# A ConvFFN trunk in float32: scaled activations from pair 6 on, and 22 pairs with seven products in place of 17

## The chip, the cores and the metric

The kernel runs on one core of a Trainium2 chip. The metric is the device time in microseconds of one execution; it is 1045.43 us before the change, the median of three runs (1045.23 to 1045.83). All data are float32, and every large matrix product is computed to nearly float32 accuracy.

## The reference

The model is an encoder trunk of two layers on 512 positions and 1024 channels. Only the second half of a layer, the ConvFFN, is touched by the change.

```python
for l in range(DEPTH):            # 2
    h = rmsnorm(x, norm1[l])
    ...
    x = x + mix @ w_o[l]

    h = rmsnorm(x, norm2[l])
    up = dwconv_centred(h @ w_up[l], conv_w[l], conv_b[l])   # 1024 -> 2 * 2816, width 3 over positions
    gate, val = up[..., :D_FF], up[..., D_FF:]
    x = x + (jax.nn.silu(gate) * val) @ w_down[l]            # 2816 -> 1024
```

The norm is x times g times a factor per position, 1 / sqrt(mean(x^2) + eps). The factor depends on the position alone, so it may be applied before the product with w_up or after it.

## The kernel before

**Layout.** Activations stand transposed: channels on the 128 partitions, the 512 positions along the free dimension. x is eight tiles x0 to x7 of 128x512. The normed input of the FFN is `h2`, eight tiles with the tag act, which hold x times norm2 without the factor of the position. The factor is a row `rb2` (tag rb), the same on all partitions; it is made last, after x is complete, from a sum of squares: `col_rstd`, then `row_rstd`, whose transposes on PE are line 242 of the profile.

**Three products for one.** Each operand is split into a high half of reduced precision and a low rest (`split`; for weights `wsplit`, tiles whi and wlo, five buffers each). The high half is a copy on ScalarE (ACT, line 94), the rest a subtraction on VectorE (DVE, line 97). `mm3` issues high x high, low x high and high x low (lines 124, 125, 126) on TensorE (PE). So each weight block costs ACT and DVE one instruction each before PE can go on. Raw weights come in loads of 512 KB into wraw, three buffers, issued by SP.

**The FFN.** The 5632 columns of w_up make 44 tiles of 128, taken as 22 pairs: gate tile fi and value tile fi + 22. The pairs stand in six groups (`GROUPS`); the down projection of a group (`rows`, eight pieces, each one output tile of x: one split of weights, 3 x 4 matmuls of 512 columns, or 3 x 3 in a group of three, and an addition to x) is interleaved with the pairs of the next group. A pair is computed in one of two ways.

- `up_eight`: two halves, gate and value, each with two splits of weights and 24 matmuls of 512 columns into one PSUM bank, then one multiplication by rb2 out of PSUM into a tile tF.
- `up_seven`: gate and value tile together as a 2 x 2 block product with seven products in place of eight, in the manner of Strassen and Winograd. It has seven splits of weights, four sums of weights (s1 to s4, into `sums` and back into wraw), 84 matmuls of 256 columns, and sums of partial results out of PSUM. On the other side it needs sums of the blocks of h, T1 to T4, which `seven_h` builds once a layer for each of four pairs of h2 tiles: two additions of halves, four sums of 256 columns, two splits into spare tiles (`h_rooms`, which hands out tiles that earlier stages of the layer have done with). At the end it multiplies by rb2: one instruction of 512 columns, two of 256.

`conv` applies the convolution over positions to the result: one ACT instruction for the centre tap and the bias, and two scalar-tensor-tensor instructions on DVE for the outer taps (line 100). SiLU runs on ACT, gate times value on DVE, and the result is split into high and low for the down projection (tiles slab and pT).

`SEVEN` lists the pairs of each layer that use `up_seven`: 7 in layer 0, 10 in layer 1. In layer 0 the same loop also prepares weights of layer 1 (`presplit`, tiles tA and m4, stored to DRAM as `kept`); `PIECES` says how many pieces each pair does.

**Order.** The program is written in this order, and a scheduler of the framework then decides each engine's instruction order from its own estimate of times, within the dependences. Each engine works through its own list in order, so an instruction that waits holds up those behind it.

## Time and profile before

| | |
|---|---|
| median of three timed runs | 1045.43 us |
| profiled execution, whole | 1045.6 us |
| its span on the core | 1043.8 us |
| PE busy | 1025.7 us, 98% |
| DVE busy | 857.2 us, 82% |
| ACT busy | 546.9 us, 52% |
| granted TensorE clock | 1.0 |

A row of the timeline reads: start in the span, duration, engine, line, operation, output<-inputs (the program's names without their numbers), shape, and in brackets how long the engine stood idle just before it and what ended that. A row of the groups reads: line, engine, operation, names, shapes and count, then busy time and mean ns of one, then the idle time just before them and what ended it. Durations of PE and DVE rows overlap the next row, so the distance from start to start is what an instruction costs its engine.

In the profiled execution rb2 is ready at about 201 us in layer 0 and 716 us in layer 1; the FFN's pairs follow.

### The profile page before, as it was taken

How to read it: one execution, taken by the hardware profiler on the slowest of the kernel's cores; microseconds unless marked ns; L12 is line 12 of the kernel's file. 1: busy time of each engine (PE TensorE's matmuls, PEld its weight loads, DVE VectorE, ACT ScalarE, POOL GpSimd, SP SyncE). 2: the span in 40 equal slices, each digit the busy share in tenths (PEclk: the TensorE clock that was granted, in tenths of full speed). 3: DMA queues.
4: the chain of work that ended last, by engine and by line, in shares of the span. 5: the costliest groups of instructions: out<-in, count | busy, mean ns of one | idle time of the engine just before them, and what ended most of it. 6: DMA issues, size and time to landing. Idle time of an engine off the chain costs nothing.

```text
span 1043.8 us, 16032 instructions
## 1 busy us (share of the span) xinstructions
PE 1025.7 (98%) x5696; PEld 888.4 (85%) x5696; DVE 857.2 (82%) x1721; ACT 546.9 (52%) x1057; POOL 61.1 (6%) x142
## 2 busy tenths in 40 slices
...
GB/s 270 89 109 68 41 93 82 116 171 189 162 199 139 196 202 207 188 200 243 226 206 219 111 62 91 132 85 98 81 101 101 115 69 134 63 127 57 111 137 81
DMA packets 64325, 140.15 MB, mean 134 GB/s; under 512 B 6386, under 2 KB 22002, under 8 KB 64244
## 3 DMA queue, kind: packets, MB, share of 16 engines
...
q14 instruction: 36, 0.29, 0.1%
...
## 4 chain that ended last, share of the span: by engine, by line
PE 90%; DVE 6%; ACT 2%; issue 1%; DMA 0%; POOL 0%; ACTq 0%; DVEq 0%; POOLq 0%
PE ps L124 27%; PE ps L126 27%; PE ps L125 27%; PE ps L122 3%; PE ps L667 2%; PE ps L660 2%; PE ps L648 1%; DVE tF L100 1%; DVE wlo L97 1%; ACT tA L94 1%; PE ps L242 1%; DVE tF L97 1%; PE ps L235 1%; DVE tA L652 1%; DVE x L97 0%
## 5 line engine op out<-in xcount | busy, mean ns | idle before, releaser
L94 ACT ACTIVATE whi<-wraw 128x512 fp32r<-128x512 f32 (+1 forms) x313 | 187.9, 614 | 230.9 <-PE ps L126 139.9
L125 PE MATMUL ps<-act,wlo 128*128 128x512 f32 (+1 forms) x700 | 250.1, 359 | 0.4 <-DVE wlo L97 0.4
L124 PE MATMUL ps<-act,whi 128*128 128x512 f32 (+1 forms) x700 | 250.5, 359 | 0.0
L126 PE MATMUL ps<-act,whi 128*128 128x512 f32 (+1 forms) x700 | 249.8, 359 | 0.0
L97 DVE TENSOR_TENSOR wlo<-wraw,whi 128x512 fp32r<-128x512 f32 (+1 forms) x321 | 210.0, 668 | 41.7 <-ACT whi L94 41.0
L125 PEld LDWEIGHTS ps<-act,wlo 128*128 128x128 f32 x700 | 132.0, 189 | 21.1 <-DVE wlo L97 1.1
L124 PEld LDWEIGHTS ps<-act,whi 128*128 128x128 f32 x700 | 132.0, 189 | 19.8
L126 PEld LDWEIGHTS ps<-act,whi 128*128 128x128 f32 x700 | 132.0, 189 | 19.2
L100 DVE SCALAR_TENSOR_TENSOR tF<-tF,pb,tF 128x511 f32<-128x511 f32 x176 | 130.2, 746 | 3.9 <-ACT tF L94 3.7
L124 PE MATMUL ps<-slab,whi 128*128 128x512 f32 (+2 forms) x274 | 105.8, 389 | 1.2 <-ACT whi L94 1.2
L125 PE MATMUL ps<-slab,wlo 128*128 128x512 f32 (+2 forms) x274 | 104.6, 382 | 0.0
L97 DVE TENSOR_TENSOR x<-x,ps 128x512 f32<-128x512 f32 (+1 forms) x113 | 75.2, 677 | 34.3 <-PE ps L126 34.0
L126 PE MATMUL ps<-slab,whi 128*128 128x512 f32 (+2 forms) x274 | 102.2, 383 | 0.3 <-DVE slab L97 0.3
L94 ACT ACTIVATE tF<-tF,pb 128x512 f32<-128x512 f32 x88 | 71.1, 811 | 29.7 <-DVE tF L97 28.0
L97 DVE TENSOR_TENSOR tF<-ps,rb 128x512 f32<-128x512 f32 (+1 forms) x87 | 54.4, 634 | 23.5 <-PE ps L126 12.2
L124 PE MATMUL ps<-room,whi 128*128 128x256 f32 x238 | 67.5, 283 | 1.1 <-ACT tF L94 1.0
L125 PE MATMUL ps<-room,wlo 128*128 128x256 f32 x238 | 67.2, 282 | 0.3 <-DVE wlo L97 0.3
L126 PE MATMUL ps<-room,whi 128*128 128x256 f32 x238 | 67.0, 282 | 0.0
L124 PE MATMUL ps<-pT,whi 128*128 128x512 f32 (+1 forms) x162 | 62.6, 388 | 0.0
L125 PE MATMUL ps<-pT,wlo 128*128 128x512 f32 (+1 forms) x162 | 62.6, 388 | 0.0
L126 PE MATMUL ps<-pT,whi 128*128 128x512 f32 (+1 forms) x162 | 61.7, 387 | 0.0
L124 PEld LDWEIGHTS ps<-slab,whi 128*128 128x128 f32 x274 | 51.5, 188 | 11.4 <-ACT whi L94 1.6
...
## 6 DMA issues: line engine op xcount, KB each, us to landing
...
```

The lines of the kernel that those rows point to most:

```text
L94: return nc.scalar.activation(out, in_, func, **kw)
L97: return (eng or nc.vector).tensor_tensor(out, a, b, op=op)
L100: return nc.vector.scalar_tensor_tensor(out=out, in0=a, scalar=s, in1=b, op0=op0, op1=op1)
L122: nc.tensor.matmul(out, a[0], b[0], start=start, stop=stop, **kw)
L124: nc.tensor.matmul(out, a[0], b[0], start=start, stop=False, **kw)
L125: nc.tensor.matmul(out, a[1], b[0], start=False, stop=False, **kw)
L126: nc.tensor.matmul(out, a[0], b[1], start=False, stop=stop, **kw)
L235: nc.tensor.matmul(pt[:, 2 * b:2 * b + 2], acc[:, b * P:(b + 1) * P], ones2, start=True, stop=True)
L242: nc.tensor.matmul(pt[:, b * P:(b + 1) * P], r[:, b:b + 1].to_broadcast([P, P]), ident, start=True, stop=True)
L648: nc.tensor.matmul(sc[:, :n], qT[p][:, e, i * P:(i + 1) * P], kT[g][:, s, j0 * P:(j1 + 1) * P], start=s == 0, stop=s == 1)
L660: tr = nc.tensor.transpose(pp[:, j * P:(j + 1) * P], pr[:, j * P:(j + 1) * P], ident)
L667: pv = nc.tensor.matmul(py[64 * e:64 * e + 64, i0 * P:(i1 + 1) * P], vp[:, j, 64 * g:64 * g + 64], pT[:, half, e, b0:b0 + 2 * (i1 - i0) + ...
```

## The change

The norm's factor goes into h itself from pair 6 on. At the start of the FFN eight new tiles `hx` take the sum of each h2 tile's halves; the code multiplies them by rb2 after pairs 2 and 3; after pair 5 the h2 tiles are split anew from hx. From pair 6 (`SCALED`) `up_eight` hands out its PSUM tile as it is, and `conv` reads PSUM three times; `up_seven` leaves out its three multiplications by rb2 and copies one block of 256 columns out of PSUM on ACT. `seven_h` takes its blocks from hx, without the two additions, and is called twice after pair 4 and twice after pair 6 (before: twice at the start, and after pairs 3 and 4). The lists of pairs with seven products grow from 7 to 10 in layer 0 and from 10 to 12 in layer 1, and the pieces of presplit are spread otherwise. At the value half of pair 5 two pieces of the down projection are taken.

```diff
--- before.py
+++ after.py
@@ -35,8 +35,10 @@
 
 GROUPS = [(0, 4), (4, 4), (8, 4), (12, 3), (15, 3), (18, 4)]
 
-PIECES = [1, 1, 2, 1, 2, 2, 2] + [1, 3] * 7 + [3]
-SEVEN = ((7, 9, 11, 13, 15, 17, 19), (6, 8, 9, 11, 12, 14, 15, 17, 18, 20))
+SCALED = 6
+
+PIECES = [1, 1, 1, 1, 1, 1, 2, 3, 1, 2, 3, 2, 1, 3, 2, 2, 3, 2, 2, 3, 2, 2]
+SEVEN = ((8, 9, 11, 12, 14, 15, 17, 18, 20, 21), (8, 9, 10, 12, 13, 14, 15, 17, 18, 19, 20, 21))
 
 
 def encoder_kernel(tc, t):
@@ -402,24 +404,26 @@
         for key, cols in zip(keys, (LO, HI)):
             g[key] = [z[:, cols] for z in two]
 
+    HX = ("th0", "th1", "tl0", "tl1", "wt0", "wt1", "v", "accA")
+
     def h_rooms():
 
-        for tag in ("th0", "th1", "tl0", "tl1", "wt0", "wt1", "v", "accA", "accF", "acc", "room"):
+        for tag in ("accF", "room"):
             yield cp.tile([P, 512], F32R, tag=tag, name=nm("room"), bufs=1)
+        for _ in range(2):
+            yield tp.tile([P, 516], F32R, tag="tail", name=nm("room"), bufs=2)[:, :512]
+        yield cp.tile([P, 512], F32R, tag="acc", name=nm("room"), bufs=1)
         yield cp.tile([P, 512], F32R, tag="rb", name=nm("room"), bufs=2)
         for _ in range(2):
-            yield tp.tile([P, 516], F32R, tag="tail", name=nm("room"), bufs=2)[:, :512]
-        for _ in range(2):
             yield temp(512, "sq", F32R)
-
-    def seven_h(k, h2, room):
-
-        b = [temp(512, "tF") for _ in range(2)]
-        for i in range(2):
-            tt(b[i], f(h2[k + 4 * i][:, 0, :]), f(h2[k + 4 * i][:, 1, :]), ALU.add)
+        for k in (0, 4, 1, 5, 2, 6, 3, 7):
+            yield cp.tile([P, 512], F32R, tag=HX[k], name=nm("room"), bufs=1)
+
+    def seven_h(k, h2, hx, room):
+
         g = dict(B11=[z[:, LO] for z in halves(h2[k])], B21=[z[:, LO] for z in halves(h2[k + 4])],
                  B22=[z[:, HI] for z in halves(h2[k + 4])])
-        t13, t24 = sums_of_b(*b)
+        t13, t24 = sums_of_b(hx[k], hx[k + 4])
         parts(g, t13, ("T1", "T3"), room)
         parts(g, t24, ("T2", "T4"), room)
         return g
@@ -432,9 +436,11 @@
             for k in range(KT):
                 mm3(o, [q[:, (k % 4) * P:(k % 4 + 1) * P] for q in w[k // 4]], [h2[k][:, s, :] for s in range(2)],
                     k == 0, k == KT - 1)
-            u = temp(512, "tF")
-            tt(u, o, rb2, ALU.mult)
-            yield u
+            if fi < SCALED:
+                u = temp(512, "tF")
+                tt(u, o, rb2, ALU.mult)
+                o = u
+            yield o
 
     def up_seven(l, fi, h2, ts, rb2):
         a, b = [wload(t["w_up"][l, fi + z * FT], 1024) for z in range(2)]
@@ -465,11 +471,9 @@
         product(X, wsplit(s3), "T3")
         tt(ub[:, HI], ub[:, HI], X, ALU.add)
         tt(ua[:, HI], ua[:, HI], Y, ALU.add)
-        tt(ua, ua, rb2, ALU.mult)
         yield ua
         product(X, wsplit(a22), "T4")
-        tt(ub[:, LO], X, rb2[:, LO], ALU.mult)
-        tt(ub[:, HI], ub[:, HI], rb2[:, HI], ALU.mult)
+        act(ub[:, LO], X)
         yield ub
 
     def conv(l, m, u):
@@ -829,7 +833,10 @@
 
         ahead = presplit(l + 1) if l < L - 1 else iter(lambda: 0, 1)
         room = h_rooms()
-        ts = [seven_h(k, h2, room) for k in range(2)]
+        hx = [cp.tile([P, 512], F32, tag=z, name=nm("hx"), bufs=1) for z in HX]
+        for k in range(KT):
+            tt(hx[k], f(h2[k][:, 0, :]), f(h2[k][:, 1, :]), ALU.add)
+        ts = []
         nxt = []
 
         def rows(f0, nf, gu):
@@ -865,12 +872,18 @@
                 ys_ = []
                 for z, u in enumerate((up_seven if fi in SEVEN[l] else up_eight)(l, fi, h2, ts, rb2)):
                     ys_.append(conv(l, fi + z * FT, u))
-                    for _ in range(-(-todo // halves_left)):
+                    for _ in range(2 if z and fi == SCALED - 1 else -(-todo // halves_left)):
                         next(down, None)
                         todo -= 1
                     halves_left -= 1
-                if fi in (3, 4):
-                    ts.append(seven_h(len(ts), h2, room))
+
+                for k in range(4 * fi - 8, 4 * fi - 4) if fi in (2, 3) else ():
+                    tt(hx[k], hx[k], rb2, ALU.mult)
+                if fi == SCALED - 1:
+                    for k in range(KT):
+                        split(h2[k][:, 0, :], h2[k][:, 1, :], hx[k])
+                for _ in range(2 if fi in (4, SCALED) else 0):
+                    ts.append(seven_h(len(ts), h2, hx, room))
                 for _ in range(PIECES[fi]):
                     next(ahead)
                 act(ys_[0], ys_[0], AF.Silu)
```

The scheduler moves instructions as well. Lines of the changed program are two higher in the helpers (99 for 97, 102 for 100, 126 to 128 for 124 to 126), numbers behind names count tiles and belong to one program alone. Three places follow.

**Behind rb2 in layer 0, on DVE.** Before, the first product of rb2 (rb_418) with a PSUM tile, and what came with it:

```order
L97 TENSOR_TENSOR wlo_515_2270<-wraw_513_2267,whi_514_2269 128x512
L97 TENSOR_TENSOR tF_441_1964<-ps_440_1939,rb_418_1891 128x512
L97 TENSOR_TENSOR tF_449_2005<-ps_448_1980,rb_418_1891 128x512
L97 TENSOR_TENSOR wlo_517_2274<-wraw_513_2267,whi_516_2273 128x512
L97 TENSOR_TENSOR tF_463_2059<-ps_462_2034,rb_418_1891 128x512
L100 SCALAR_TENSOR_TENSOR tF_442_1966<-tF_441_1964,pb_96,tF_442_1966 128x511
```

After it the convolution of the first pair began. In the changed program the first such product (tF_433<-ps_432) is followed by seven multiplications of hx tiles, and then by these rows:

```order
L99 TENSOR_TENSOR hx_425_1899<-hx_425_1899,rb_418_1891 128x512
L99 TENSOR_TENSOR wlo_504_2248<-wraw_500_2241,whi_503_2247 128x512
L99 TENSOR_TENSOR hx_426_1900<-hx_426_1900,rb_418_1891 128x512
L99 TENSOR_TENSOR tF_441_1985<-ps_440_1960,rb_418_1891 128x512
L102 SCALAR_TENSOR_TENSOR tF_434_1946<-tF_433_1944,pb_96,tF_434_1946 128x511
L99 TENSOR_TENSOR wlo_516_2304<-wraw_514_2301,whi_515_2303 128x512
L99 TENSOR_TENSOR wlo_518_2308<-wraw_514_2301,whi_517_2307 128x512
```

All eight multiplications of hx by rb2 now stand between the first PSUM tile's and the second's, with one split of weights among them.

**Pair 5 to pair 6 in layer 0, on DVE.** Before, in the order of the program, the additions of the previous group's down pieces to x, a sum for T parts, and the low halves of the weights of a down piece (wlo_596) and of the next pair (wlo_609, wlo_611, wlo_617):

```order
L97 TENSOR_TENSOR x1_75<-x1_75,ps_556_2445 128x512
L97 TENSOR_TENSOR x2_76<-x2_76,ps_586_2547 128x512
L97 TENSOR_TENSOR tF_559_2463<-tF_558_2460,tF_557_2459 128x256
L97 TENSOR_TENSOR wlo_596_2603<-wraw_583_2541,whi_595_2602 128x512
L97 TENSOR_TENSOR wlo_609_2645<-wraw_607_2642,whi_608_2644 128x512
L97 TENSOR_TENSOR wlo_611_2649<-wraw_607_2642,whi_610_2648 128x512
L97 TENSOR_TENSOR wlo_617_2686<-wraw_615_2683,whi_616_2685 128x512
```

The changed program has the same down piece as wlo_579 and the next pair as wlo_588 and wlo_590. The low halves of the eight h2 tiles, split anew, stand in the 24 rows ahead of them, the last two here:

```order
L99 TENSOR_TENSOR act_408_1849<-hx_425_1899,act_408_1849 128x512
L99 TENSOR_TENSOR x1_75<-x1_75,ps_536_2407 128x512
L99 TENSOR_TENSOR x2_76<-x2_76,ps_565_2509 128x512
L99 TENSOR_TENSOR act_412_1871<-hx_426_1900,act_412_1871 128x512
L99 TENSOR_TENSOR wlo_579_2585<-wraw_577_2582,whi_578_2584 128x512
L99 TENSOR_TENSOR wlo_588_2635<-wraw_586_2632,whi_587_2634 128x512
```

So all eight low halves are written ahead of the down piece's weights.

On PE the down piece (ps_597) and the first product of pair 6 (ps_612, which reads the h2 tile act_370) stood thus before:

```order
L124 MATMUL ps_597_2606<-slab_456_2021,whi_595_2602 128x512
L124 MATMUL ps_612_2652<-act_370_1689,whi_608_2644 128x512
L124 MATMUL ps_618_2689<-slab_456_2021,whi_616_2685 128x512
L125 MATMUL ps_597_2606<-slab_456_2021,wlo_596_2603 128x512
L126 MATMUL ps_597_2606<-slab_456_2021,whi_595_2602 128x512
```

and the changed program has, with ps_580 for the down piece and ps_591 for pair 6:

```order
L126 MATMUL ps_580_2588<-slab_448_2001,whi_578_2584 128x512
L126 MATMUL ps_591_2642<-act_370_1689,whi_587_2634 128x512
L126 MATMUL ps_595_2675<-slab_448_2001,whi_593_2671 128x512
L127 MATMUL ps_580_2588<-slab_448_2001,wlo_579_2585 128x512
L128 MATMUL ps_580_2588<-slab_448_2001,whi_578_2584 128x512
```

PE's order is the same here. Between rb2's transposes and the first use of the down piece's low half PE has 209 matmuls of 512 columns in the changed program's layer 0 and 201 in its layer 1.

**A seven pair late in layer 1, on DVE.** Before, the end of pair 17 (tF_2164 is its gate tile, tF_2165 its value tile) with multiplications by rb2 (rb_1680), and splits and sums of weights of pair 18:

```order
L97 TENSOR_TENSOR tF_2165_10103<-tF_2165_10103,ps_2161_10099 128x256
L100 SCALAR_TENSOR_TENSOR tF_2179_10212<-tF_2164_10102,pb_96,tF_2179_10212 128x511
L97 TENSOR_TENSOR wlo_2202_10305<-wraw_2192_10277,whi_2201_10304 128x512
L97 TENSOR_TENSOR x7_81<-x7_81,ps_2189_10259 128x512
L97 TENSOR_TENSOR tF_2165_10103<-tF_2165_10103,rb_1680_7567 128x256
L97 TENSOR_TENSOR wlo_2204_10322<-wraw_2191_10275,whi_2203_10321 128x512
L97 TENSOR_TENSOR wlo_2206_10340<-sums_2200_10301,whi_2205_10339 128x512
L97 TENSOR_TENSOR tF_2165_10103<-ps_2161_10099,rb_1680_7567 128x256
L97 TENSOR_TENSOR wraw_2191_10275<-wraw_2191_10275,sums_2200_10301 128x512
L100 SCALAR_TENSOR_TENSOR tF_2186_10251<-tF_2165_10103,pb_96,tF_2186_10251 128x511
```

The changed program at the same place (tF_2169 is the value tile of pair 17, tF_2200 the gate tile of pair 18):

```order
L99 TENSOR_TENSOR tF_2169_10260<-tF_2169_10260,ps_2165_10256 128x256
L99 TENSOR_TENSOR x7_81<-x7_81,ps_2193_10414 128x512
L99 TENSOR_TENSOR wlo_2206_10460<-wraw_2196_10432,whi_2205_10459 128x512
L99 TENSOR_TENSOR wlo_2208_10477<-wraw_2195_10430,whi_2207_10476 128x512
L99 TENSOR_TENSOR wlo_2210_10495<-sums_2204_10456,whi_2209_10494 128x512
L99 TENSOR_TENSOR wraw_2195_10430<-wraw_2195_10430,sums_2204_10456 128x512
L102 SCALAR_TENSOR_TENSOR tF_2190_10406<-tF_2169_10260,pb_96,tF_2190_10406 128x511
L99 TENSOR_TENSOR tF_2200_10437<-tF_2200_10437,ps_2199_10436 128x256
L99 TENSOR_TENSOR wlo_2212_10513<-wraw_2195_10430,whi_2211_10512 128x512
```

The rows with rb are gone; the first tap (tF and pb) has only the sum out of PSUM ahead of it.

In the whole program 128x512 matmuls go from 2732 to 2492 and 128x256 matmuls from 1708 to 2128. On DVE the additions for hx, the multiplications of hx by rb2 and the low halves of the new split are 16 each over both layers; 16 additions of seven_h, 30 multiplications of a whole PSUM tile by rb2, and all 17 + 17 + 17 of the seven pairs go; each of the five more seven pairs has four sums and three splits of weights more, and the taps that read PSUM are 40. On ACT the copies of 256 columns out of PSUM go from 51 to 88, and the splits of weights by 15 more.

## The prediction

> **What bounds the kernel now.** I read the page's first part, its chain of work that ended last, then the windows, then the timeline of PE and of DVE, and last the groups of instructions by form.
>
> ```profile
> span 1043.8 us, 16032 instructions
> PE 1025.7 (98%) x5696; PEld 888.4 (85%) x5696; DVE 857.2 (82%) x1721; ACT 546.9 (52%) x1057; POOL 61.1 (6%) x142
> PE 90%; DVE 6%; ACT 2%; issue 1%; DMA 0%; POOL 0%; ACTq 0%; DVEq 0%; POOLq 0%
> ```
>
> PE carries 90% of the chain that ends last, DVE 6%. The change lies in the FFN alone, so the FFN's own windows count, one over most of layer 0's and one late in layer 1's (columns: stretch, its length, busy PE, PEld, DVE, ACT, POOL, granted clock, DMA share, GB/s; the third row counts only instructions that touch the tA tiles, which presplit uses):
>
> ```profile
> 202.00:470.00 268.00, 267.14 (x1444) 231.92 (x1443) 249.79 (x447) 147.57 (x259) 0.00 (x0) 1.00 0.56 184
> 850.00:875.00 25.00, 25.00 (x161) 22.77 (x160) 21.43 (x38) 13.13 (x23) 0.00 (x0) 1.00 0.41 126
> 202.00:470.00 268.00, 0.00 (x0) 0.00 (x0) 30.81 (x71) 19.54 (x35) 0.00 (x0) 1.00 0.56 184
> ```
>
> PE is full in both at a granted clock of 1.00; DVE is close behind at 249.79/268 = 93% in layer 0, where presplit takes 30.81/22 pairs, at least 1.3 us a pair, and at 86% late in layer 1. So two prices matter: what a matmul costs PE from start to start, and what an instruction costs DVE from start to start (a row's own duration holds a tail that overlaps the next).
>
> ```profile
> 419.80 0.39 PE L124 MATMUL ps<-act,whi 128*128 128x512 f32 x1
> ...
> 432.49 0.39 PE L126 MATMUL ps<-pT,whi 128*128 128x512 f32 x1
> 432.71 0.28 PE L124 MATMUL ps<-act,whi 128*128 128x256 f32 x1
> ...
> 437.37 0.28 PE L124 MATMUL ps<-room,whi 128*128 128x256 f32 x1
> ```
>
> From 419.80 to 432.71 lie 57 starts of 512 columns, .2265 us each (I use .2267, which longer stretches gave); from 432.71 to 437.37 lie 39 of 256, .1195 each. DVE, back to back:
>
> ```profile
> 962.00 0.42 DVE L97 TENSOR_TENSOR tF<-ps,rb 128x256 f32<-128x256 f32 x1
> 962.34 0.68 DVE L97 TENSOR_TENSOR wraw<-wraw,sums 128x512 f32<-128x512 f32 x1
> ...
> 964.91 0.75 DVE L100 SCALAR_TENSOR_TENSOR tF<-tF,pb,tF 128x511 f32<-128x511 f32 x1
> 965.57 0.69 DVE L97 TENSOR_TENSOR wlo<-sums,whi 128x512 fp32r<-128x512 f32 x1
> 966.17 0.55 DVE L97 TENSOR_TENSOR wlo<-wraw,whi 128x384 fp32r<-128x384 f32 x1
> 966.64 0.69 DVE L97 TENSOR_TENSOR tF<-tF,tF 128x512 f32<-128x512 f32 x1
> ```
>
> So a 512 tensor-tensor takes .60 us of DVE, a 256 one .34, a 384 one .47, and one tap of the convolution .66.
>
> **The change part by part.** *Five more pairs with seven products.* The order has 240 matmuls of 512 columns fewer and 420 of 256 more. While PE is packed: 240 x .2267 = 54.4 us less, 420 x .1195 = 50.2 more, net **-4.2 us**, .85 for each pair.
>
> *Does DVE allow it?* An eight pair without its down pieces was 4 splits, 2 multiplications by rb2, gate times value and its low half (8 x .60) and 4 taps (2.64): 7.4 us; two down pieces add 4 x .60: 9.8, beside PE's 48 x .2267 + 24 x .2267 = 16.3. A seven pair was 7 splits, 4 sums, the whole rb2 multiplication, product and low half (14 x .60), 5 of 256 (1.7), 4 taps and the down pieces: 15.1, beside PE's 84 x .1195 + 5.4 = 15.5. That left no room in layer 0, where presplit comes on top. From pair 6 on each pair loses 1.2 us of DVE: a seven pair needs 13.9 (15.2 with presplit), an eight pair 8.6. So runs of sevens fit, and in layer 0, where no run is longer than two, an eight between them leaves DVE 16.3 - 8.6 - 1.3 = 6.4 us over. The multiplications that go save no time on PE; they buy this cover.
>
> *Convolution from PSUM and the copies on ACT.* Three reads of a PSUM tile in place of one multiplication and three reads of SBUF.
>
> ```profile
> L100 DVE SCALAR_TENSOR_TENSOR tF<-tF,pb,tF 128x511 f32<-128x511 f32 x176 | 130.2, 746 | 3.9 <-ACT tF L94 3.7
> L100 DVE SCALAR_TENSOR_TENSOR act<-ps,pa,act 128x512 fp32r<-128x512 f32 x8 | 6.0, 746 | 5.1 <-ACT act L94 5.1
> L94 ACT ACTIVATE tF<-tF,pb 128x512 f32<-128x512 f32 x88 | 71.1, 811 | 29.7 <-DVE tF L97 28.0
> ```
>
> The same kind of instruction takes 746 ns from SBUF and 746 ns from PSUM, so the 40 moved taps cost nothing more by these rows; the ends are nothing and, if the next instruction could not overlap such a tap's tail (.746 - .66 = .09 us), 40 x .09 = 3.6 us of DVE. They begin behind the re-split, where DVE has room beside PE. [...] ACT gains 68 instructions net (16 high halves of the re-split, 37 copies out of PSUM, 15 splits of weights), at most .81 us each by the last row, 55 us; it is at 52% and in layer 0 at 147.57/268 = 55%, and the cover would be gone only where one of them stands ahead of a split that PE waits for. I take nothing. The PSUM bank is released after the second tap, not after one multiplication, about 1.5 us later; six banks rotate, a use every 2.7 us (12 matmuls) to 5.4 us (24), so nothing.
>
> *hx, from h2's halves and rb2.* Eight additions a layer, eight multiplications right behind rb2, eight re-splits after pair 5; the 16 additions of seven_h go. The additions lie ahead of rb2, in place of 16 instructions of seven_h, and DVE stands idle 1.52 us there (next rows, in brackets): nothing. The multiplications and re-splits lie in the one stretch in which DVE is already late: nothing of the first pairs can be multiplied before rb2, so a backlog forms there.
>
> ```profile
> 200.10 1.05 PE L242 MATMUL ps<-ident,nr 128*128 128x128 f32 x8
> 200.91 0.48 PE L125 MATMUL ps<-act,wlo 128*128 128x512 f32 x1
> ...
> 201.82 1.29 DVE L97 TENSOR_TENSOR tF<-ps,rb 128x512 f32<-128x512 f32 x2 [1.52 <-ACT rb L94]
> ```
>
> The transposes that spread rb2 hold PE .81 us, and the first multiplication starts 1.72 us after their first. Layer 0 after, by the order: from that multiplication through the low half of the down piece behind the re-split DVE has 83 instructions, 52 of 512, 20 taps, 6 of 256, 5 of 384: 31.2 + 13.2 + 2.0 + 2.4 = 48.8, and with 1.72 and .1 for the last one's tail 50.6 us behind the transposes. PE, with 209 matmuls of 512 in between, asks at .81 + 47.4 = 48.2. **Stall 2.4 us.** Layer 1: 76 instructions (49, 20, 7 of 256) give 45.0 + 1.8 = 46.8; PE asks after 201 matmuls, at 46.4. **Stall .4.** The overwritten h2 tiles add no wait of their own: their last readers on PE lie at least 25 matmuls (5.7 us) ahead.
>
> How good is this count? On before, the same sum can be compared with what happened at the first seven pair of layer 1:
>
> ```profile
> 716.88 1.89 DVE L97 TENSOR_TENSOR tF<-ps,rb 128x512 f32<-128x512 f32 x3 [0.84 <-ACT rb L94]
> 763.22 0.28 PE L124 MATMUL ps<-act,whi 128*128 128x256 f32 x1
> 764.47 0.38 PE L124 MATMUL ps<-room,whi 128*128 128x256 f32 x1 [0.97 <-ACT tF L94]
> 765.16 0.39 PE L125 MATMUL ps<-room,wlo 128*128 128x256 f32 x1 [0.30 <-DVE wlo L97]
> 765.38 0.28 PE L126 MATMUL ps<-room,whi 128*128 128x256 f32 x1
> ...
> 769.20 0.29 PE L124 MATMUL ps<-act,whi 128*128 128x256 f32 x1
> 769.99 0.50 PE L124 MATMUL ps<-slab,whi 128*128 128x512 f32 x1 [0.50 <-ACT whi L94]
> 770.35 0.39 PE L125 MATMUL ps<-act,wlo 128*128 128x256 f32 x1
> ```
>
> The 80 DVE instructions in between (51 of 512, 21 taps, 8 of 256) make 47.2 us by these prices and end at 764.1; PE's wait ended at 765.16, so DVE's own waits were 1.0 us, 2%. In before they were waits for PE and ACT; with a longer backlog fewer inputs are late, so I take half: .5 more in each layer. New stalls: 2.9 + .9 = **+3.8 us**, with ends of 2.8 and 4.8.
>
> *Stalls that go.* In these rows PE lost 765.38 - 763.22 - 3 x .12 = 1.8 us and 770.35 - 769.20 - .12 - .23 = .8, together 2.6. Both places have an eight pair now, and the backlog is paid at the re-split. In layer 0 the first seven pair lost .4:
>
> ```profile
> 270.59 0.39 PE L124 MATMUL ps<-slab,whi 128*128 128x512 f32 x1
> 271.10 0.38 PE L124 MATMUL ps<-room,whi 128*128 128x256 f32 x1
> 271.32 0.28 PE L125 MATMUL ps<-act,wlo 128*128 128x256 f32 x1
> ...
> 371.99 0.39 PE L124 MATMUL ps<-act,whi 128*128 128x256 f32 x1
> 373.02 0.49 PE L124 MATMUL ps<-slab,whi 128*128 128x512 f32 x1 [0.65 <-ACT whi L94]
> 373.60 0.39 PE L125 MATMUL ps<-act,wlo 128*128 128x256 f32 x1
> ```
>
> That makes **-3.0**. The second place here, 1.61 - .35 = 1.3 us lost at a later seven pair, I leave as it is: one such place before, one after. Sum: -4.2 + 3.8 - 3.0 = **-3.4 us**. The profiled execution's time is 1045.6 us (1.8 around the span), the median of the timed runs 1045.43, .2 lower; I forecast 1045.43 - 3.4 = **1042.0**.
>
> **The rivals.** (a) *The cover is enough everywhere.* If the waits hide behind ACT's and PE's own order and the re-split costs PE nothing, the sum is -4.2 - 3.0, and with the 1.3 at 371.99 gone as well -8.5: 1037 to 1038. For it: late in layer 1 DVE loses 1.2 of 15.1 us a pair. Against: the count that places the backlog fell short of the measured one, not beyond it. (b) *The backlog is paid in full and goes on*: DVE's 2% in both layers, and the first sevens still find DVE late, because the last two groups of T parts are now built after pair 6. Stalls 4.8, and 2.0 of the 3.0 do not go: -4.2 + 4.8 - 1.0 = -.4, 1045.0. For it: in layer 0, four groups of T parts are built between pairs 4 and 8, with presplit beside them. Against: pairs 6 and 7 are eights, where DVE has 6.4 us over. (c) *Slower: each seven pair of layer 0 repeats the stall of 371.99.* There a presplit fold stood on DVE between a seven pair's sums and its splits. Ten sevens at 1.3, less the 1.7 that the old ones lost: 1042.0 + 11.3 = 1053.3. It decides against no change from 3.4/10 = .34 us lost per seven pair. Against: six of before's seven did not show it, with 1.2 us more DVE each. (d) *The product count buys nothing because PE is not the bound*: -4.2 falls away, and the time is within .5 of 1045.4; 90% of the chain on PE speaks against it.
>
> **How the numbers follow.** Forecast (1040.5 to 1043.3) .50; (a) .12; (b) and (d) together .28; (c) .10. The likeliest's time is 1042.0. The range, 1038.5 to 1046.0, takes in the ends of the stalls and (b), and leaves out most of (a) and all of (c). A measurement of this kernel can tell about 0.2%, 2.1 us. Faster by more than that (under 1043.3): .50 + .12, and nothing of the rest, .62. Within 0.2%: .29. Slower: .09, nearly all of (c).
>
> **What would show it.** In the changed profile: 2732 - 240 matmuls of 512 columns, and PE's starts still .2267 and .1195 apart late in both layers; a PE wait for DVE of 2 to 4 us at the down pieces behind pair 5 in layer 0 and about 1 in layer 1, with DVE without idle time from rb2 to there; no wait of over 1 us at the first seven pair; the taps from PSUM at 746 ns. I am wrong in the sum if that wait is under 1 or over 5 us, and in the mechanism if PE waits in the middle of runs of seven pairs, above all with a presplit fold or a load named as releaser.

## The result, and the profile after

The changed kernel took 1055.44 us (median of five runs, 1054.45 to 1057.25) beside 1045.43 for the kernel before. The ratio is 1.0094, with a 95% interval of 1.0082 to 1.0106: **slower by 10.0 us, where 1042.0 was forecast**, and outside the range of 1038.5 to 1046.0. The profiled execution took 1055.45 us.

The page's first rows and the chain of work that ended last:

```profile
span 1053.7 us, 16487 instructions
PE 1029.4 (98%) x5876; PEld 894.6 (85%) x5876; DVE 862.7 (82%) x1722; ACT 569.0 (54%) x1125; POOL 61.5 (6%) x142
PE 83%; DVE 8%; ACT 4%; DMA 3%; issue 1%; POOL 0%; ACTq 0%; DVEq 0%; POOLq 0%
```

PE's share of the chain fell from 90% to 83%; DVE, ACT and a DMA have taken its place. PE's busy time rose from 1025.7 to 1029.4 us although its matmuls should cost less. The busy time of a matmul is no measure here (512 columns are .39 to .63 us long in the rows below, at starts .2267 us apart where PE is packed), so the tables below use distances from start to start: whatever a distance has above .2267 us for 512 columns and .1195 for 256 is a wait (or a slow clock), summed by me over all PE rows of a stage's timeline; the rest is work.

| kernel | median us | PE work | waits, FFN layer 0 | waits, FFN layer 1 |
|---|---|---|---|---|
| before | 1045.43 | 0 | 2.9 | 4.1 |
| changed | 1055.44 | -4.2 | 15.0 | 6.7 |

-4.2 + 12.1 + 2.6 = 10.5, against 9.9 of span; the attention stages' waits are nearly the same in sum. The gain of the matmuls is there in full, and the waits outweigh it more than three times. The first large one is the re-split of layer 0, here in PE's timeline:

```profile
248.64 0.39 PE L128 MATMUL ps<-slab,whi 128*128 128x512 f32 x1
249.78 0.47 PE L126 MATMUL ps<-slab,whi 128*128 128x512 f32 x1 [0.76 <-DVE x L99]
250.98 0.47 PE L126 MATMUL ps<-act,whi 128*128 128x512 f32 x1 [0.73 <-DVE x L99]
251.58 0.47 PE L126 MATMUL ps<-slab,whi 128*128 128x512 f32 x1
252.69 0.49 PE L127 MATMUL ps<-slab,wlo 128*128 128x512 f32 x1 [0.64 <-DVE wlo L99]
...
253.73 0.63 PE L127 MATMUL ps<-slab,wlo 128*128 128x512 f32 x1
254.16 0.63 PE L128 MATMUL ps<-slab,whi 128*128 128x512 f32 x1
254.59 0.63 PE L126 MATMUL ps<-slab,whi 128*128 128x512 f32 x1
```

Between 248.64 and 252.69 PE starts four matmuls in the time of 18 and loses 3.15 us, at the place that was forecast (ps_580, the first use of wlo_579) with 2.9. The first two of its waits ended with additions to x on DVE, which empty PSUM banks, and the last one with the low half: all of it is DVE's backlog. But behind it the matmuls start .43 us apart and not .2267. The windows show why, in the third column from the end (granted clock):

```profile
250.00:252.00 2.00, 1.14 (x3) 0.37 (x2) 2.00 (x5) 0.44 (x1) 0.00 (x0) 1.00 0.00 0
252.00:254.00 2.00, 1.36 (x5) 1.08 (x5) 2.00 (x5) 0.13 (x1) 0.00 (x0) 0.79 0.00 0
254.00:256.00 2.00, 2.00 (x6) 1.52 (x6) 2.00 (x5) 0.51 (x1) 0.00 (x0) 0.50 0.24 19
256.00:258.00 2.00, 2.00 (x9) 1.66 (x8) 2.00 (x4) 0.78 (x2) 0.00 (x0) 0.85 0.94 313
```

The granted clock falls to .50 and costs another 1.7 us before it is back. DVE (third count) has no idle time in these rows. In layer 1 the re-split's wait is 1.9 us and the clock stays at 1; here the last part of it ended with ACT, and the rows of ACT show why:

```profile
768.51 0.39 PE L126 MATMUL ps<-slab,whi 128*128 128x512 f32 x1
769.09 0.47 PE L126 MATMUL ps<-act,whi 128*128 128x512 f32 x1 [0.19 <-DVE tF L99]
769.59 0.50 PE L126 MATMUL ps<-slab,whi 128*128 128x512 f32 x1
770.98 0.50 PE L126 MATMUL ps<-slab,whi 128*128 128x512 f32 x1 [0.88 <-ACT whi L96]
```

```profile
768.75 1.65 ACT L96 ACTIVATE act<-hx 128x512 fp32r<-128x512 f32 x3
770.31 0.61 ACT L96 ACTIVATE whi<-wraw 128x512 fp32r<-128x512 f32 x1
```

Three high halves of the re-split (act<-hx) stand on ACT right ahead of the high half that PE needs.

The old waits at the first seven pairs are gone. The rest of the loss stands in runs of seven pairs, where before had next to nothing, and at the end of layer 0's FFN. Layer 0 waits .9 us at pair 12, .7 at 15, 3.1 at 18, 1.5 at 21; layer 1 waits .4 at pair 19, 2.0 at 20, 1.2 at 21. Some 2 us more come at the end of layer 0's FFN, half of them for weights that presplit had prepared:

```profile
530.08 0.41 PE L126 MATMUL ps<-whi,act 128*128 128x384 f32 x1 [1.10 <-DMA whi<-kept]
```

Pair 20 of layer 1, first PE, then ACT, then DVE:

```profile
998.04 0.28 PE L128 MATMUL ps<-act,whi 128*128 128x256 f32 x1
998.85 0.38 PE L126 MATMUL ps<-room,whi 128*128 128x256 f32 x1 [0.53 <-ACT whi L96]
999.37 0.39 PE L126 MATMUL ps<-act,whi 128*128 128x256 f32 x1
999.72 0.39 PE L127 MATMUL ps<-room,wlo 128*128 128x256 f32 x1
```

```profile
992.17 0.63 ACT L96 ACTIVATE whi<-wraw 128x512 fp32r<-128x512 f32 x1 [2.33 <-DMA wraw<-in_w_up_dram]
...
997.47 0.82 ACT L96 ACTIVATE tF<-tF,pb 128x512 f32<-128x512 f32 x1
998.19 1.13 ACT L96 ACTIVATE whi<-wraw 128x512 fp32r<-128x512 f32 x2
```

```profile
994.81 0.68 DVE L99 TENSOR_TENSOR sums<-wraw,wraw 128x512 f32<-128x512 f32 x1
995.41 0.75 DVE L102 SCALAR_TENSOR_TENSOR tF<-tF,pb,tF 128x511 f32<-128x511 f32 x1
996.08 0.68 DVE L99 TENSOR_TENSOR x<-x,ps 128x512 f32<-128x512 f32 x1
996.68 0.68 DVE L99 TENSOR_TENSOR wraw<-wraw 128x512 f32<-128x512 f32 x1
```

PE stands at 998.04 because the weights of the second product (a sum of two raw tiles) are not split: ACT's high half starts at 998.19, behind a convolution's centre tap; DVE's sum was made at 996.68, behind a tap and an addition to x of other tiles; and ACT had waited 2.33 us for the pair's raw weights. Their loads wait for buffers that the low halves before them free; over the whole kernel this is what the queue of the loads waits for most, as it was in the kernel before (340.8 us in 71 waits):

```profile
SPq L135 <- DVE wlo L99: 362.2, 81, 13.2
```

(us in total, times, longest.) It is a chain of three engines in which each has a little other work ahead of the needed piece.

In layer 0 the chain starts late too. The first sums of the raw weights of pairs 12 and 15:

```profile
347.23 0.69 DVE L99 TENSOR_TENSOR sums<-wraw,wraw 128x512 f32<-128x512 f32 x1 [1.51 <-DMA wraw<-in_w_up_dram]
400.16 0.69 DVE L99 TENSOR_TENSOR sums<-wraw,wraw 128x512 f32<-128x512 f32 x1 [1.67 <-DMA wraw<-in_w_up_dram]
```

DVE stood idle for the loads there, so it was not simply full. Over all 22 seven pairs of this trace the distance from that sum to the pair's first matmul tells the pairs apart: it is .8 to 3.1 us in the eight pairs in which PE waited (.4 us or more; pair 9 of layer 0 is among them) and 4.3 us or more in the fourteen others. In six of the eight DVE stood idle for the raw weights, .6 to 1.7 us, right before the sum.

### The profile page after: what moved, and what is told of

Same layout as the page of the kernel before. It is cut to its first block, busy times and chain, and to the rows that moved or that the text cites. A ratio compares the mean times of both kernels' runs of the same rounds, so it can differ in the third digit from the quotient of the medians.

```text
span 1053.7 us, 16487 instructions
## 1 busy us (share of the span) xinstructions
PE 1029.4 (98%) x5876; PEld 894.6 (85%) x5876; DVE 862.7 (82%) x1722; ACT 569.0 (54%) x1125; POOL 61.5 (6%) x142
## 4 chain that ended last, share of the span: by engine, by line
PE 83%; DVE 8%; ACT 4%; DMA 3%; issue 1%; POOL 0%; ACTq 0%; DVEq 0%; POOLq 0%
PE ps L126 25%; PE ps L127 24%; PE ps L128 24%; DMA wraw<-in_w_up_dram 3%; PE ps L124 3%; PE ps L671 2%; DVE wlo L99 2%; PE ps L664 2%; DVE tF L102 1%; PE ps L652 1%; ACT whi L96 1%; DVE act L99 1%; ACT tA L96 1%; DVE x L99 1%; ACT act L96 1%
## 5 line engine op out<-in xcount | busy, mean ns | idle before, releaser
L99 DVE TENSOR_TENSOR wlo<-wraw,whi 128x512 fp32r<-128x512 f32 (+1 forms) x326 | 212.8, 669 | 51.5 <-ACT whi L96 50.1
L126 PE MATMUL ps<-act,whi 128*128 128x512 f32 (+1 forms) x680 | 237.3, 349 | 1.6 <-DVE x L99 0.7
L127 PE MATMUL ps<-act,wlo 128*128 128x512 f32 (+1 forms) x680 | 236.4, 349 | 0.6 <-DVE wlo L99 0.6
L128 PE MATMUL ps<-act,whi 128*128 128x512 f32 (+1 forms) x680 | 236.0, 348 | 0.0
L126 PEld LDWEIGHTS ps<-act,whi 128*128 128x128 f32 x680 | 128.4, 189 | 20.3 <-ACT whi L96 2.4
L127 PEld LDWEIGHTS ps<-act,wlo 128*128 128x128 f32 x680 | 128.4, 189 | 18.3 <-DVE wlo L99 1.5
L128 PEld LDWEIGHTS ps<-act,whi 128*128 128x128 f32 x680 | 128.4, 189 | 16.3
L102 DVE SCALAR_TENSOR_TENSOR tF<-tF,pb,tF 128x511 f32<-128x511 f32 x136 | 100.8, 747 | 1.5 <-ACT tF L96 1.0
L126 PE MATMUL ps<-room,whi 128*128 128x256 f32 x308 | 88.1, 286 | 3.8 <-ACT whi L96 2.0
L127 PE MATMUL ps<-room,wlo 128*128 128x256 f32 x308 | 87.0, 282 | 0.0
L128 PE MATMUL ps<-room,whi 128*128 128x256 f32 x308 | 86.6, 281 | 0.0
L126 PEld LDWEIGHTS ps<-room,whi 128*128 128x128 f32 x308 | 58.3, 189 | 6.9 <-ACT tF L96 3.5
L96 ACT ACTIVATE tF<-tF,pb 128x512 f32<-128x512 f32 x68 | 54.9, 808 | 10.6 <-DVE tF L99 10.2
```

The lines of the kernel that those rows point to most:

```text
L96: return nc.scalar.activation(out, in_, func, **kw)
L99: return (eng or nc.vector).tensor_tensor(out, a, b, op=op)
L102: return nc.vector.scalar_tensor_tensor(out=out, in0=a, scalar=s, in1=b, op0=op0, op1=op1)
L126: nc.tensor.matmul(out, a[0], b[0], start=start, stop=False, **kw)
L127: nc.tensor.matmul(out, a[1], b[0], start=False, stop=False, **kw)
L128: nc.tensor.matmul(out, a[0], b[1], start=False, stop=stop, **kw)
```

## The experiments

The first four cut the change in two and take away one suspected cause each. In diffs, lines of the changed kernel are marked -, unless said otherwise.

**scale_old_lists**, the scaling alone:

```diff
-PIECES = [1, 1, 1, 1, 1, 1, 2, 3, ...]
-SEVEN = ((8, 9, 11, ...), (8, 9, 10, ...))
+PIECES = [1, 1, 2, 1, 2, 2, 2] + [1, 3] * 7 + [3]
+SEVEN = ((7, 9, 11, 13, 15, 17, 19), (6, 8, 9, 11, 12, 14, 15, 17, 18, 20))
-                for _ in range(2 if fi in (4, SCALED) else 0):
+                for _ in range(2 if fi in (4, SCALED - 1) else 0):
```

> The scaled activations alone: the lists of seven pairs and the presplit pieces are those of before (17 pairs), the rest is the changed kernel (seven_h is called after pairs 4 and 5, since layer 1 has a seven pair at 6). Theory 1, the backlog in front of the re-split and the slow clock behind it make part of the loss, and runs of seven pairs the rest: the stall of about 3 us with a granted clock near 0.5 behind it stays in layer 0, some 2 us stay in layer 1, the old stalls of 3 us at the first seven pairs go, little else: about 1047 to 1050 us. Theory 2, the loss is all from the runs of seven pairs: 1045 us or less. Theory 3, it is all from the scaling: 1055 plus the 4 us of the missing seven pairs, 1059 us.

Measured: 1066.51 us, ratio 1.0199 [1.0184, 1.0215]. No theory had it. The re-split's wait and slow clock are there (5.4 us), but right behind it PE waits another 5.9 us in layer 0 and, with the re-split's, 13.6 in layer 1. With a seven pair at 6 or 7 the T parts stand in the same backlog as the re-split. The run shows that a seven pair right behind the re-split waits; the shares it was made for it does not show.

**lists_only**, the lists alone, in the kernel before:

```diff
-PIECES = [1, 1, 2, 1, 2, 2, 2] + [1, 3] * 7 + [3]
-SEVEN = ((7, 9, 11, 13, 15, 17, 19), (6, 8, 9, 11, 12, 14, 15, 17, 18, 20))
+PIECES = [1, 1, 1, 1, 1, 1, 2, 3, 1, 2, 3, 2, 1, 3, 2, 2, 3, 2, 2, 3, 2, 2]
+SEVEN = ((8, 9, 11, 12, 14, 15, 17, 18, 20, 21), (8, 9, 10, 12, 13, 14, 15, 17, 18, 19, 20, 21))
```

> The kernel before with the lists of the changed one (22 seven pairs, its presplit pieces), and every up projection still multiplied by rb2. Theory 1: no backlog in front of pair 6, so no slow clock; the matmuls save 4.2 us, but each second pair of a run waits for its weights as in the changed kernel or more, since DVE has 1.2 us a pair more to do: some 10 to 12 us of waits, about 1051 us. Theory 3, the scaling makes all of the loss: 1041 to 1043 us.

Measured: 1065.72 us, ratio 1.0194 [1.0179, 1.0210]. PE's work falls by 4.2 us as it should, and the waits are 21.1 us in layer 0 and 11.4 in layer 1, nearly three times what I expected. They stand in the runs, but for 5.4 us at the end of layer 0's FFN. So the new lists alone lose 20 us, and the scaling gives half of it back: theory 3 falls.

**rescale_later**, the re-split one pair later:

```diff
-SCALED = 6
+SCALED = 7
```

> SCALED is 7: the re-split stands after pair 6 and pair 6 is still multiplied by rb2, so the backlog has an eight pair more to drain. Theory 1: the waits in front of the re-split (3.2 us in layer 0, 1.9 in layer 1) and the 1.7 us of slow clock go, the waits in the runs stay: 1055.4 - 6.8 = about 1049 us. Rival, the backlog only moves on to the re-split wherever it stands: 1054 to 1057 us, with a wait and a slow clock one pair later.

Measured: 1064.27 us, ratio 1.0181 [1.0164, 1.0198]. The wait at the re-split is gone in both layers, as theory 1 has it. But the last T parts are now built after pair 7, right ahead of the seven pair 8, and PE waits 9.7 us there in layer 0. The time went against the theory, the mechanism for it.

**wraw_four**:

```diff
-             "tA": (512, 6), ... "m4": (1024, 5)
+             "tA": (512, 6), ... "m4": (1024, 4)
-        return wp.tile([P, 1024], F32, tag="wraw", name=nm("wraw"))
+        return wp.tile([P, 1024], F32, tag="wraw", name=nm("wraw"), bufs=4)
```

> The changed kernel with four buffers for raw weights in place of three (and four for the tiles m4 in place of five, to make room). Theory 1, the second pair of a run waits because its loads cannot start before the first pair frees its buffers: the waits behind 300 us in layer 0's runs (some 6 us) and behind 980 us in layer 1 (some 4 us) nearly go, about 1046 us. Rival, DVE and ACT are what is late there (presplit in layer 0, the longer chain of sums): the waits stay and so does the time, 1054 to 1056 us.

Measured: 1058.84 us, ratio 1.0126 [1.0111, 1.0141]. In layer 1 the waits of the late run fall from 3.7 to 1.2 us (and 1.9 come at its very end); in layer 0 those of pairs 18 to 21 stay at about 4.4. In layer 0 those of pairs 12 and 15 fall from 1.6 to .4 us. The attention stages lose 5 to 6 us, which I put to the missing m4 tile; no run shows it. So the loads are part of the chain in both layers. Pair 18 of layer 0 still waits 1.5 us of its 3.1, and something else may stand in front there: in the changed kernel its first load is issued at 441.86 us, behind five of presplit's stores in SP's order, and SP had waited 6.8 us for the first of their tiles.

The next four ask whether the waits belong to the place of the runs, and what the backlog is. **scale_on_pool**:

```diff
-                    tt(hx[k], hx[k], rb2, ALU.mult)
+                    tt(hx[k], hx[k], rb2, ALU.mult, nc.gpsimd)
-                        split(h2[k][:, 0, :], h2[k][:, 1, :], hx[k])
+                        split(h2[k][:, 0, :], h2[k][:, 1, :], hx[k], eng=nc.gpsimd)
```

> The changed kernel, with the eight multiplications of hx by rb2 and the eight low halves of the re-split on GpSimd (POOL) in each layer, where it stands idle. Theory 1, DVE's backlog between rb2 and the re-split makes the waits there and the slow clock behind them: 16 x .60 = 9.6 us of DVE go from a stretch that is 3.2 us (layer 0) and 1.9 us (layer 1) late, so these waits and the 1.7 us of slow clock go, 1055.4 - 6.8 = about 1049 us, if POOL needs less than about 3 us for one. Rival, something else is late there (the x additions that free PSUM banks, or the re-split itself, which POOL would do more slowly): 1055 us or more, PE then waits for POOL.

Measured: 1064.54 us, ratio 1.0185 [1.0168, 1.0202]. Its groups on POOL:

```profile
L99 POOL TENSOR_TENSOR act<-hx,act 128x512 fp32r<-128x512 f32 x16 | 28.9, 1839 | 56.7 <-ACT act L96 56.6
L99 POOL TENSOR_TENSOR hx<-hx,rb 128x512 f32<-128x512 f32 x16 | 26.3, 1675 | 12.3 <-ACT rb L96 12.3
```

POOL needs 1.84 us for one low half, and the eight stand together, 241.8 to 257.6 us. The wait with its slow clock grows to 9.4 us. DVE's backlog was not tested by it, only moved to a slower engine.

**no_late_runs**:

```diff
-SEVEN = ((8, 9, 11, 12, 14, 15, 17, 18, 20, 21), (8, 9, 10, 12, 13, 14, 15, 17, 18, 19, 20, 21))
+SEVEN = ((8, 9, 11, 12, 14, 15, 17, 20), (8, 9, 10, 12, 13, 14, 15, 17, 20))
```

> The changed kernel with 17 seven pairs, all runs of the changed lists kept up to pair 17, but from 18 on only pair 20 (5 of the 22 are eight pairs again: 18 and 21 in layer 0, 18, 19 and 21 in layer 1). Theory 4, the waits in runs come from pairs 18 to 21, where the down pieces beside a pair have 9 matmuls and not 12, so that PE needs 14.1 us a seven pair and DVE 13.6 (14.9 with presplit): the waits of 4.6 us (layer 0) and 3.7 us (layer 1) there go, PE's work rises by 4.2 us: 1051 us. Theory 1 in its first form (every second pair of a run waits for its loads): the waits at pairs 12 and 15 stay too and the layer 1 runs up to 17 show none, as now; same time, so the next run tells them apart.

Measured: 1047.25 us, ratio 1.0017 [1.0008, 1.0027], faster than expected. Its times spread from 1045.73 to 1049.22 us, and the profiled execution is the fastest of them. The same stretch of layer 0 in the changed kernel, then in this one:

```profile
300.00:530.00 230.00, 225.75 (x1338) 198.59 (x1336) 206.83 (x375) 132.48 (x248) 1.56 (x6) 1.00 0.60 201
```

```profile
300.00:530.00 230.00, 230.00 (x1297) 201.97 (x1296) 203.25 (x366) 132.32 (x243) 1.44 (x6) 1.00 0.62 210
```

PE is full. Left are the re-split's 4.9 and 1.4 us. The waits at pairs 12 and 15, whose neighbourhood the edit does not touch, are gone too, but for .3 us.

**late_runs**:

```diff
+SEVEN = ((8, 10, 12, 14, 17, 18, 20, 21), (8, 10, 12, 14, 17, 18, 19, 20, 21))
```

> The changed kernel with 17 seven pairs, alternate ones up to pair 14 and the changed lists' run from 17 on in both layers. Theory 4: the waits at pairs 18 to 21 stay (8.3 us), those at 12 and 15 (1.6 us) go, PE's work rises by 4.2 us: 1058 us. Rival (waits come from how many seven pairs there are, not where): half the waits, 1054 us.

Measured: 1058.45 us, ratio 1.0124 [1.0099, 1.0148]. The time is theory 4's, in part by luck. The kernel is 11 us slower than no_late_runs with the same number of seven pairs, but the late pairs have only 5.3 us of waits where the theory had 8.3: 3.2 us at pairs 19 to 21 of layer 1, close to the changed kernel's 3.7 (no_late_runs has none), and 2.1 at pairs 18 and 21 of layer 0. The rest are 2.4 us at the end of layer 0's FFN, 2.2 us that were lost before rb2 of layer 0 (202.8 beside 200.6 us), ahead of anything the edit names, and, not foreseen, 3.9 us at the lone seven pair 12 of layer 0 (356 to 362 us), some 2 of them a wait and the rest a granted clock of .65 to .78 behind it. Against these stand 1.6 us less at the re-split.

**groups_moved**:

```diff
-GROUPS = [(0, 4), (4, 4), (8, 4), (12, 3), (15, 3), (18, 4)]
+GROUPS = [(0, 4), (4, 4), (8, 4), (12, 4), (16, 3), (19, 3)]
```

> The changed kernel with groups of 4, 4, 4, 4, 3, 3 pairs in place of 4, 4, 4, 3, 3, 4, so that the eight down pieces of 9 matmuls fall beside three pairs (19 to 21) and not four: PE needs 15.5 us a seven pair there, and 17.3 in pairs 16 to 18. Theory 4: the waits from pair 18 on (8.3 us) nearly go, 1047 to 1049 us. Rival (load release or presplit, whatever the group): they stay, 1054 to 1057 us.

Measured: 1054.78 us, ratio 1.0085 [1.0070, 1.0100]. Layer 1's late waits fall from 3.7 to .9 us, and 1.1 come at its very end; in layer 0 those from pair 18 on fall from 4.6 to 3.2 only, and 3 us come at pairs 8 and 9. The time is the rival's. The waits go half theory 4's way in layer 1, and in layer 0 more PE work beside the late pairs does not suffice; that presplit is the reason is not shown.

The next four try to remove the re-split's wait from no_late_runs, and to see what the scaling is worth there. **resplit_after_6** (against no_late_runs):

```diff
-SCALED = 6
+SCALED = 7
-                for _ in range(2 if fi in (4, SCALED) else 0):
+                for _ in range(2 if fi in (4, SCALED - 1) else 0):
```

> The kernel no_late_runs (17 seven pairs, the changed lists without the runs from pair 18 on) with SCALED 7 and the last two groups of T parts called after pair 6: the re-split stands one eight pair later and seven_h's sums still have pair 7 in front of the first seven pair. Theory 1: DVE's backlog is drained before the re-split (the order has its work end 4 us ahead of PE's first use there in layer 0, where it was 2.4 late), so no wait and no slow clock there and none at pair 8: 1047.3 - 4.9 - 1.4 = about 1041 us. Rival: the backlog is there wherever the re-split stands: 1047 us or more, as in the run with SCALED 7, whose 9.7 us at the first seven pair were then not due to the T parts' place.

Measured: 1047.10 us, ratio 1.0015 [1.0006, 1.0024]. Its windows over the old place of the re-split and over the first seven pair of layer 0:

```profile
240.00:262.00 22.00, 22.00 (x99) 18.22 (x98) 22.00 (x41) 14.14 (x26) 0.00 (x0) 1.00 0.48 150
280.00:295.00 15.00, 11.08 (x72) 9.43 (x71) 15.00 (x29) 10.46 (x21) 0.00 (x0) 1.00 0.40 125
```

The re-split costs PE nothing now, in layer 1 as well (waits of .56 and .40 us are all that is left there); in layer 0 DVE is still late one and a half pairs later, at the seven pair, and PE waits 5.7 us. In layer 0 the backlog moved, in layer 1 it was drained, and the time is that of no_late_runs, as the rival has it. Presplit is the work that layer 0 has and layer 1 has not; that it makes the difference this run alone does not show.

**resplit_after_6_pieces** (against the last one):

```diff
-PIECES = [1, 1, 1, 1, 1, 1, 2, 3, 1, 2, 3, 2, 1, 3, 2, 2, 3, 2, 2, 3, 2, 2]
+PIECES = [0, 0, 0, 0, 0, 0, 3, 3, 1, 2, 4, 2, 1, 3, 2, 2, 4, 2, 3, 4, 2, 3]
```

> The same with the six pieces of presplit of pairs 0 to 5 moved to pairs 6 to 21, most to eight pairs. Theory 1: nothing waits in front of the re-split any more, so the pieces' place gives nothing there, and DVE has up to 1.2 us a pair more later on: 1041 us, or up to 2 us more. Rival (presplit is what makes DVE late): faster than the run without this edit by over 2 us.

Measured: 1047.68 us, ratio 1.0022 [1.0013, 1.0032]: no gain; 4.2 us of waits at the first seven pair in place of 5.7, and 1.8 more later. In the time the first six pieces' place does not matter.

**late_sums_pieces** (against no_late_runs): these pieces, and

```diff
-                for _ in range(2 if fi in (4, SCALED) else 0):
+                for _ in range(2 if fi in (SCALED, SCALED + 1) else 0):
```

> no_late_runs with the re-split left after pair 5, but the T parts built after pairs 6 and 7 and the pieces of pairs 0 to 5 moved later. By the order DVE's work up to the re-split falls from 48.8 to 47.5 us and its lateness from 2.4 to .9 us: the PE wait there falls from 3.2 to about 1.5 us and the slow clock goes (about 3 us less), if the clock follows the length of the wait; the T parts now stand in front of the first seven pair, which costs some of it: 1044 to 1048 us. Rival (the clock falls there whatever the wait): granted clock still near 0.5 for 3 us.

Measured: 1053.02 us, ratio 1.0078 [1.0061, 1.0094]. The wait at the re-split is 1.6 us and the clock stays at 1.00 there, as expected; the T parts ahead of the first seven pair cost 4.8 us, with the clock at .50 behind them, more than expected.

**before_early_runs**: the kernel before with the lists of no_late_runs.

> The kernel before (every product multiplied by rb2, no re-split) with the lists and pieces of no_late_runs: 17 seven pairs, as before, but in runs. Theory 1 (the scaled activations buy DVE the room for runs): no wait at a re-split, but waits in the runs that no_late_runs does not have, 5 us or more in layer 0, about 1050 us. Rival (the scaled activations buy nothing, the place of the seven pairs does it): 1041 to 1043 us, no_late_runs without its re-split wait.

Measured: 1048.49 us, ratio 1.0026 [1.0015, 1.0038]. Waits of 9.3 us in layer 0 (6.4 in no_late_runs, 4.9 of them the re-split's) and 1.4 in layer 1. The two kernels differ by 1.2 us, and their times overlap. In layer 0 the scaling takes the waits out of the runs and puts a similar sum at the re-split; in layer 1 runs of three and four up to pair 17 need no scaling.

What was open now was how the layers share the loss, and whether long runs need the scaling. The last five keep layer 0 as in the kernel before. **scale_layer1_only** has the scaling in layer 1 alone, with the changed list:

```diff
+SCALED = (99, 6)
+SEVEN = ((7, 9, 11, 13, 15, 17, 19), (8, 9, 10, 12, 13, 14, 15, 17, 18, 19, 20, 21))
-            if fi < SCALED:
+            if fi < SCALED[l]:
...
```

> Layer 0 as in the kernel before (its 7 seven pairs, its presplit pieces, rb2 behind every product), layer 1 as in the changed kernel (scaled activations from pair 6, 12 seven pairs). Theory 1 and 4: PE's work falls by 2 x .85 = 1.7 us, layer 0 keeps its 2.9 us of waits, layer 1 has the changed kernel's 6.7 in place of 4.1: 1045.5 - 1.7 + 2.6 = about 1046.4 us; nearly all of the changed kernel's loss is layer 0's. Rival, the loss is shared by both layers: 1050 us.

Measured: 1046.41 us, ratio 1.0006 [.9998, 1.0015], to a tenth as expected. Of the changed kernel's loss about 9 us are layer 0's.

**scale_layer1_later**:

```diff
-SCALED = (99, 6)
-SEVEN = (..., (8, 9, 10, 12, 13, 14, 15, 17, 18, 19, 20, 21))
+SCALED = (99, 7)
+SEVEN = (..., (8, 9, 10, 12, 13, 14, 15, 16, 17, 18, 20))
+                for _ in range((2 if fi in (4, SCALED[l] - 1) else 0) if scaled else ...):
```

> Layer 0 as before; layer 1 scaled with the re-split after pair 6, T parts called after pairs 4 and 6, and 11 seven pairs with no run from 18 on (8, 9, 10, 12 to 18, 20). Theory: layer 1's waits fall to about 1.7 us (as in resplit_after_6) from 4.1, the work by .85: 1045.5 - 2.4 - .9 = about 1042.3 us. Rival, the run of seven seven pairs from 12 to 18 waits for its loads: 1046 us.

Measured: 1043.15 us, ratio .9976 [.9967, .9984]: **faster than both kernels**. The run of seven pairs from 12 to 18 shows one wait of .3 us and no other.

**before_layer1_runs**, the kernel before with one list changed:

```diff
-SEVEN = (..., (6, 8, 9, 11, 12, 14, 15, 17, 18, 20))
+SEVEN = (..., (8, 9, 10, 12, 13, 14, 15, 17, 18, 20))
```

> The kernel before with one edit: layer 1's ten seven pairs are 8, 9, 10, 12 to 15, 17, 18, 20 (before: 6, 8, 9, 11, 12, 14, 15, 17, 18, 20). No scaling. Theory: no seven pair at 6, so DVE's backlog behind rb2 drains and the 2.7 us of waits at 763 to 771 us go; the waits in runs stay below 1 us as in before_early_runs: 1043 us. Rival (runs of three and four wait without the scaling): 1046 us.

Measured: 1043.64 us, ratio .9982 [.9973, .9991]. Pairs 6 and 11 have given way to 10 and 13, and no seven pair stands in the backlog behind rb2 any more: the waits of 1.8 and .9 us at 763 to 771 us are gone, and the edit is worth 2 us.

**before_layer1_dense** (the same with 8 to 18 and 20):

> The same with 12 seven pairs in layer 1 (8 to 10, 11 to 18, 20 without a gap up to 18). Theory: another 1.7 us of PE work less; DVE needs 15.1 us a pair beside PE's 15.5 and no eight pair gives it room, so waits of some 2 to 5 us come: 1043 to 1046 us. Rival (layer 1 has room for any run as long as presplit is not beside it): 1041.5 us.

Measured: 1052.02 us, ratio 1.0065 [1.0051, 1.0079]: 10.6 us of waits in layer 1, more than I expected.

**scale_layer1_dense**, the same list with the scaling of scale_layer1_later:

> scale_layer1_later with one seven pair more in layer 1 (11), so that its list is that of before_layer1_dense: 8 to 18 without a gap, and 20. The two kernels differ only in the scaling of layer 1 (from pair 7 on, re-split after pair 6). Theory (the scaling buys the room for runs): the 10.6 us of waits in layer 1 of before_layer1_dense fall to 2 to 4, 1042 to 1044 us. Rival (a run this long waits for its loads or its chains whatever DVE has to do): 1050 to 1052 us.

Measured: 1042.53 us, ratio .9968 [.9956, .9981], the lowest median of all, though its interval overlaps that of scale_layer1_later. On one list the scaling takes the waits of layer 1 from 10.6 to 2.4 us and the time from 1052.02 to 1042.53. The stretch of the run, without and with:

```profile
820.00:970.00 150.00, 143.64 (x968) 131.74 (x968) 137.26 (x243) 76.71 (x143) 0.00 (x0) 1.00 0.28 89
```

```profile
820.00:970.00 150.00, 150.00 (x1024) 139.50 (x1023) 136.83 (x232) 85.84 (x160) 0.00 (x0) 1.00 0.34 104
```

56 matmuls more in the same time, and PE full, though DVE is busy for the same share of it: 136.83 and 137.26 of 150 us. Beside the best list without the scaling (before_layer1_runs, 1043.64 us) the scaling is worth about 1 us.

## Why the prediction was wrong, point by point

**The five more seven pairs: right.** PE's work fell by 4.2 us in every kernel with the changed lists.

**The taps from PSUM: right.** In the groups of the changed kernel they take what they took from SBUF:

```profile
L102 DVE SCALAR_TENSOR_TENSOR tF<-ps,pb,tF 128x511 f32<-128x511 f32 x40 | 29.8, 746 | 3.2 <-ACT tF L96 3.2
```

The 40 taps from PSUM mean 746 ns, the 136 from SBUF 747, and from start to start both take .66 us. So the 3.6 us of DVE that the prediction gave as the taps' far end did not come.

**The re-split: place right, the wait right in layer 0 and too short in layer 1, price too low.** It is 3.15 us against 2.9 in layer 0 and 1.9 against .9 in layer 1. DVE's own waits between rb2 and the re-split were .4 us in each layer, close to the half that was taken, so they do not explain layer 1. There ACT comes in, whose added work the sum had put at nothing; it would matter only where an instruction of it "stands ahead of a split that PE waits for", and three high halves of the re-split did. DVE's low half was ready at 770.74 us and ACT's high half at 770.92, one matmul earlier in PE's order, which makes about .5 us. I priced the wait at its length. Behind it the granted clock fell to .50 for some 3.5 us, 1.7 us more, a term the sum did not have. It fell behind a stretch of 4 us that was not idle but had four matmuls in it. The length of the wait alone does not decide it, and what does, no run here shows. In groups_moved the same place lost 3.25 us and the clock stayed at 1.00:

```profile
252.00:254.00 2.00, 1.46 (x6) 1.24 (x7) 2.00 (x4) 0.27 (x1) 0.00 (x0) 1.00 0.00 0
254.00:256.00 2.00, 2.00 (x10) 1.63 (x9) 2.00 (x5) 0.36 (x1) 0.00 (x0) 1.00 0.26 34
```

**The stalls that go: right.** The 2.6 us of layer 1's first seven pair and the .4 of layer 0's are gone.

**"Does DVE allow it?": the step that failed.** It said that "runs of sevens fit" because a seven pair needs 13.9 us of DVE (15.2 with presplit) beside PE's 15.5, and left the later stalls "as it is: one such place before, one after". Measured are 6.2 us of waits in layer 0's runs, 3.7 in layer 1's and some 2 at the end of layer 0's FFN. In layer 1 the sentence held for the runs up to pair 15, and it failed at pairs 19 to 21; in layer 0 the second pair of each run from pair 12 on waited. Two things were wrong in it.

First, the 5.4 us of down pieces in PE's 15.5 are 2 pieces of 12 matmuls. From pair 15 on the pieces come from groups of three pairs and have 9, and in pairs 18 to 20 two of them give PE 84 x .1195 + 18 x .2267 = 14.1 us, beside 13.6 of DVE (their splits have 384 columns) and 14.9 with presplit. That is .5 us of room in layer 1 and less than none in layer 0. no_late_runs, with one late seven pair in each layer, has no wait in late pairs, and late_runs, with the same number of seven pairs, has 5.3 us of them: so the place counts, though these waits are only half of the 11 us between the two kernels.

Second, it took a sum of DVE's time that stays just below PE's for enough; in layer 0 that was 15.2 beside 15.5 us. A seven pair's splits hang on a chain (load, sum on DVE, high half on ACT, low half on DVE, each behind other work in its engine's order), which can be late though no engine is full. The windows of the changed kernel's layer 1 over two pairs that did not wait (13, 14), and over the ones before and at the wait (19, 20):

```profile
880.86:899.68 18.82, 18.82 (x119) 17.03 (x118) 15.89 (x27) 8.73 (x17) 0.00 (x0) 1.00 0.32 91
899.68:915.13 15.45, 15.45 (x111) 14.51 (x110) 14.41 (x24) 9.24 (x17) 0.00 (x0) 1.00 0.34 105
...
979.39:994.81 15.42, 15.30 (x107) 14.20 (x106) 14.56 (x25) 8.75 (x17) 0.00 (x0) 1.00 0.30 101
994.81:1011.61 16.80, 15.78 (x107) 14.18 (x106) 14.12 (x25) 9.50 (x18) 0.00 (x0) 1.00 0.27 85
```

DVE is at 15.89/18.82 = 84% in the first and 14.56/15.42 = 94% in the second, just ahead of the wait. But the share draws no border: pair 14, which did not wait, stood at 93% (14.41 of 15.45), and the runs of scale_layer1_dense and before_layer1_dense at 91 and 92%, the first with no idle time of PE and the second with 6.4 us of it. What tells the pairs of the changed kernel apart is how long before the pair's first matmul its first sum is made (.8 to 3.1 us, or 4.3 and more).

**The rivals.** (c), with 1053.3 us and a chance of .10, came nearest, and in part for its reason: in layer 0 seven pairs do wait, with presplit beside them. But it is not each seven pair, the long wait stands late in the runs, and layer 1 has its share without presplit; that its time is only 2 us off is in part luck. Its threshold held: the ten seven pairs of layer 0 lost .6 us each on average, above the .34 from which it was to decide. (a) is refuted by the wait at the re-split, and (b) by the first seven pair of each layer, which shows no wait. (d) is refuted by the work term. What I argued against (c), that six of seven pairs had shown no stall before, was drawn from pairs that each had an eight pair in front.

**What stays open.** Why the waits of layer 0 at pairs 12 and 15 go in no_late_runs, where these pairs are the same, and why the lone seven pair 12 waits in late_runs. Each edit of a list makes the scheduler set the whole layer anew, so an edit is never one change alone; nothing was tried that keeps the order fixed. How much of the waits in the runs is loads and how much DVE and ACT is open as well: in layer 1 four load buffers and more PE work per pair each took away about half or more, and in layer 0 the loads also stand behind presplit's stores, which no run takes away alone.
